# Two transformer blocks on one core: keys transposed once, fewer compressed-score matmuls, a new head, a lag of three

## The chip, the cores and the metric

The kernel runs on one core of a Trainium2 chip. The metric is device time of one execution in microseconds (us); less is better. Below, TensorE is PE in the profile (its weight loads PEld), VectorE is DVE, ScalarE is ACT, GpSimd is POOL and SyncE is SP.

## The reference

256 tokens of 1024 features go through a first block of two layers and a second one of two layers; everything is fp32.

```python
def first_block(x, mem, ...):
    mem_n = rms_norm(mem, mem_norm_g)
    for i in range(2):
        h = rms_norm(x, g_mix_pre[i])
        proj = h @ w_in[i]                       # q 12 heads, k and v 3 heads, 4 memory queries, 64 each
        tok = mixer_a(...) if i == 0 else mixer_b(...)   # banded with sinks | normed, axial rotary, full
        mkv = mem_n @ w_mem_kv[i]
        mo = memory_attention(qm, km, vm)
        x = x + rms_norm(concat(tok, mo) @ w_o[i], g_mix_post[i])
        h = rms_norm(x, g_ffn_pre[i])
        gu = h @ w_gate_up[i]                    # 2 x 2816
        f = (silu(gu[..., :2816]) * gu[..., 2816:]) @ w_down[i]
        x = x + rms_norm(f, g_ffn_post[i])
    return x

def second_block(x, ...):
    for l in range(2):
        x = x + 0.5 * swiglu(rmsnorm(x, ffn1_norm[l]), ...)      # 2816 wide
        h = rmsnorm(x, mix_norm[l]) @ w_in[l]
        h_a, h_b, h_c = split(h)
        o = concat(mla_mixer(h_a), nsa_mixer(h_b), diff_mixer(h_c))   # latent, sparse, differential
        x = x + o @ w_out[l]
        x = x + 0.5 * swiglu(rmsnorm(x, ffn2_norm[l]), ...)
    return rmsnorm(x, final_norm)
```

In `nsa_mixer` each of six query heads scores 15 compressed keys of its group, then all blocks of keys and a window of keys.

## The kernel before

**Numbers.** Every fp32 operand of a product is split into two fp32r tiles, hi and lo, and a product is three matmuls: hi by hi, hi by lo and lo by hi (`mm3`, line 554). A weight unit of 128x1024 numbers comes by DMA from SP into one of three `raw` buffers; ScalarE copies it to `hi`, VectorE subtracts to get `lo` (`load`, line 619), and there are seven pairs of those.

**Two halves.** The tokens are two halves of 128, A and B, each a generator (`script`, line 1485) that asks for weight units in the same order. `drive` (line 1518) gives each unit to A and, `LAG` = 4 units later, to B. Pieces of attention (generators that yield between steps) are advanced once a unit. So while A is at the end of a stage and its norm runs on VectorE and ScalarE, TensorE works on B's last units of the stage before.

**Order of the work.** The program is run once with a `Recorder` (line 98) that notes every engine call with what it reads and writes; `plan` (line 179) lays them out in time with a model of each call's duration (`cost`, line 445) and of the tile slots, and `Replay` (line 399) issues them in that order. So all of the profile's lines of the kernel's body are L417, the helper's. In `plan` each engine takes what is ready in program order (`MODE` = "order"); on VectorE and ScalarE a ready call gives way to one that comes ready soon. `either` lets plan choose between VectorE and ScalarE for a copy. The instructions of `setup` (line 814), among them the identities idf (fp32), idr (fp32r) and idb (bf16), are not in the plan.

**Keys.** `k_split` (line 715) writes hi, lo and hi again side by side, 192 columns a head. `k_stack` (line 725) transposes columns 0 to 127 (hi over lo) and 64 to 191 (lo over hi), two transposes a head, and one copy of 128x256 moves both to SBUF. One matmul of the stacked query (hi over lo) with each stack then gives hi by hi plus lo by lo, and hi by lo plus lo by hi. The second block's sparse keys go the same way in `mix_2`, into `KN`. In `compressed` (line 1280) a head takes two matmuls of 16 columns, one for each stack of `KC`, added up in PSUM on a mask that a matmul of 96 columns has put there.

**The head.** `memory_kv` (line 898) loads 128 rows of `mem` and the gain (512 KB each), multiplies them, transposes the product (`norm_t`, `trsplit`), and projects with `w_mem_kv`. SP issues both loads, and behind them the weight units.

**Ends of a stage.** `add_normed` (line 657) squares the two accumulators on ScalarE, takes the root's reciprocal on GpSimd, and on VectorE scales and adds to x; then `norm_t` multiplies x by the next gain, and PE transposes it. There are four such ends a half in the first block. `add_scaled` (line 665) does the second block's without a norm.

## Time and profile before

| | |
|---|---|
| Runs, us | 1672.1, 1673.17, 1675.07 (median 1673.17) |
| Profiled execution: span from first to last instruction, us | 1670.2 |
| Time of the profiled execution by the clock of the runs | not given beside the span; the median is 3.0 above the span |
| PE busy, us (share of the span) | 1645.6 (99%) |
| DVE, ACT busy | 1031.5 (62%), 895.1 (54%) |
| Mean granted clock of PE | 0.998 |
| Chain of waits that ended last | PE 93%, DVE 3%, DMA 2%, ACT 1%, issue 1% |

A matmul's end in the profile is modelled and reaches into the next one's time, so that what one costs in a row of them is read from start to start. A row with xN is N instructions in succession. The idle time in brackets is that of the engine before the row, with what ended it. The granted clock is 1.00 at 2.4 GHz; 0.50 is 1.2 GHz.

### The profile page before, as it was taken

The numbers are of one execution on the slowest core, as the hardware profiler recorded it, in microseconds if no ns is written. First come the engines' busy times: TensorE is split into PE (matmuls) and PEld (weight loads), VectorE is DVE, ScalarE is ACT, GpSimd is POOL, SyncE is SP. The second block draws the span as 40 slices with busy tenths as digits, with TensorE's granted clock in tenths as the row PEclk, the third lists the DMA queues.
The fourth block names the chain that finished last, engine by engine and source line by source line (L and its number), as shares of the span: only waits on it lengthen the run. The fifth ranks groups of instructions, "written<-read, shape, count | busy, mean of one in ns | idle before, by whom it ended". The sixth has DMA issues, their size and how long they took to land.

```text
span 1670.2 us, 23044 instructions
## 1 busy us (share of the span) xinstructions
PE 1645.6 (99%) x8648; PEld 1381.4 (83%) x8648; DVE 1031.5 (62%) x1731; ACT 895.1 (54%) x1531; POOL 42.1 (3%) x54
## 2 busy tenths in 40 slices
PE   7999999999999999999999999999999999999998
PEld 6888888789788878888899888888888889888886
DVE  6768555586655565554787755546555588765544
ACT  5766444466544354453677644435454477654443
POOL 0000000010000010000000000000000000000000
PEclk9999999999999999999999999999999999999999
DMA  7526665442566556665533366656665543356653
GB/s 256 177 65 178 182 208 187 154 159 77 171 187 204 186 166 190 185 200 180 161 106 115 114 180 185 192 188 178 181 203 183 170 128 119 103 152 181 196 184 106
DMA packets 141970, 277.12 MB, mean 166 GB/s; under 512 B 19681, under 2 KB 49441, under 8 KB 141857
## 3 DMA queue, kind: packets, MB, share of 16 engines
q1 hardware_dynamic: 141856, 275.64, 54.3%
q8 instruction: 68, 1.11, 0.3%
q14 instruction: 46, 0.37, 0.1%
HBM read 274.55 MB, written 1.05 MB: 165 GB/s over the span
## 4 chain that ended last, share of the span: by engine, by line
PE 93%; DVE 3%; DMA 2%; ACT 1%; issue 1%; POOL 0%; SPq 0%; POOLq 0%; ACTq 0%; DVEq 0%
PE acc L417 86%; PE tr L417 7%; DVE lo L417 1%; DVE tmp L417 1%; DMA raw<-in_w_mem_kv 1%; ACT hi L417 1%; DMA qkg<-in_qk_norm_g 0%; DVE tiny L417 0%; POOL tiny L417 0%; DVE x L417 0%; DMA raw<-in_w_in 0%; ACT tmp L417 0%; DMA f<-in_nsa_phi_v 0%; SPq L417 0%; DVE big L417 0%
## 5 line engine op out<-in xcount | busy, mean ns | idle before, releaser
L417 DVE TENSOR_TENSOR lo<-raw,hi 128x1024 fp32r<-128x1024 f32 (+3 forms) x510 | 609.3, 1197 | 499.7 <-ACT hi L417 498.9
L417 PE MATMUL acc<-hi,hT 128*128 128x512 f32 (+4 forms) x2944 | 876.3, 375 | 1.5 <-ACT hi L417 0.5
L417 ACT ACTIVATE hi<-raw 128x1024 fp32r<-128x1024 f32 (+3 forms) x510 | 528.8, 1039 | 602.8 <-PE acc L417 545.7
L417 PEld LDWEIGHTS acc<-hi,hT 128*128 128x128 f32 x2944 | 537.4, 189 | 99.4 <-DVE hT L417 2.6
L417 PE MATMUL acc<-lo,hT 128*128 128x512 f32 (+4 forms) x1472 | 552.2, 376 | 4.2 <-DVE lo L417 3.9
L417 PE MATMUL acc<-hi,big 128*128 128x512 f32 (+1 forms) x1360 | 398.2, 396 | 0.0
L417 PEld LDWEIGHTS acc<-lo,hT 128*128 128x128 f32 x1472 | 277.5, 189 | 52.7 <-DVE lo L417 6.6
L417 PEld LDWEIGHTS acc<-hi,big 128*128 128x128 f32 (+1 forms) x1360 | 251.4, 188 | 51.2 <-ACT big L417 0.3
L417 PE MATMUL acc<-lo,big 128*128 128x512 f32 (+1 forms) x680 | 223.0, 396 | 0.0
L417 ACT ACTIVATE tmp<-acc,tiny 128x256 f32<-128x256 f32 (+4 forms) x272 | 133.9, 502 | 36.7 <-PE acc L417 26.3
L417 PEld LDWEIGHTS acc<-lo,big 128*128 128x128 f32 (+1 forms) x680 | 127.2, 188 | 27.0 <-issue 0.3
L417 PE MATMUL tr<-idf,tmp 128*128 128x128 f32 x796 | 128.0, 275 | 9.6 <-DVE tmp L417 7.5
L417 PEld LDWEIGHTS tr<-idf,tmp 128*128 128x128 f32 x796 | 98.6, 143 | 29.5 <-issue 8.4
L417 ACT ACTIVATE big<-tr 128x512 fp32r<-128x512 f32 (+3 forms) x192 | 88.2, 474 | 49.7 <-PE tr L417 46.1
L417 POOL TENSOR_TENSOR tiny<-tiny,nhalf 128x1 f32<-128x1 f32 (+4 forms) x46 | 39.5, 859 | 1605.4 <-DVE tiny L417 1565.4
L417 DVE TENSOR_TENSOR big<-tr,big 128x512 fp32r<-128x512 f32 (+3 forms) x108 | 61.0, 572 | 16.5 <-ACT big L417 13.1
L417 PE MATMUL acc<-v,tmp 128*128 128x64 f32 x520 | 68.4, 267 | 0.0
L417 PEld LDWEIGHTS acc<-v,tmp 128*128 128x128 f32 x520 | 66.9, 192 | 1.5 <-issue 0.3
L417 DVE SCALAR_TENSOR_TENSOR tmp<-acc,tiny,tmp 128x512 f32<-128x512 f32 x72 | 50.6, 703 | 14.4 <-PE acc L417 13.9
L417 DVE TENSOR_REDUCE tiny<-acc 128x2 f32<-128x512 f32 (+2 forms) x76 | 49.4, 651 | 11.1 <-PE acc L417 9.9
L417 PE MATMUL acc<-big,big 128*128 128x256 f32 (+1 forms) x232 | 45.0, 302 | 0.0
L417 PEld LDWEIGHTS tr<-idr,tmr 128*128 128x128 f32 x340 | 37.0, 142 | 8.1 <-DVE tmr L417 3.5
(134 smaller groups left out, 714.8 us busy)
## 6 DMA issues: line engine op xcount, KB each, us to landing
raw<-in_w_gate_up SPq DMA_DIRECT2D x88, 512.0 KB, 3.7
raw<-in_ffn_wg SPq DMA_DIRECT2D x88, 512.0 KB, 3.7
raw<-in_ffn_wu SPq DMA_DIRECT2D x88, 512.0 KB, 3.7
raw<-in_ffn_wd SPq DMA_DIRECT2D x88, 512.0 KB, 3.3
raw<-in_w_down SPq DMA_DIRECT2D x44, 512.0 KB, 3.4
raw<-in_w_in SPq DMA_DIRECT2D x20, 512.0 KB, 3.7
raw<-in_w_in SPq DMA_DIRECT2D x24, 384.0 KB, 3.3
raw<-in_w_o SPq DMA_DIRECT2D x16, 512.0 KB, 3.3
```

The source lines that it names most:

```text
L417: getattr(getattr(self.nc, eng), name)(*args, **kw)
```

## The change

It has five parts. (1) `k_split` writes hi and lo once; a key head has one transpose, and the new `halves` makes the second stack by copying the upper 64 partitions to the lower ones and the reverse: three copies in place of one. `KN` is filled the same way. (2) `compressed` scores a head with one matmul of 32 columns (both stacks side by side, mask of 192 columns), and VectorE adds the two halves. (3) `memory_kv` loads `mem` and the gain in halves of 256 KB with the first weight unit requested in between, and `script` puts 16 matmuls of idb by idb (256 columns) ahead of everything. (4) `LAG` is 3. (5) `plan` makes four passes. In the first every engine goes by program order; each pass gives every call a latest start, reckoned back from TensorE's sequence without gaps, and in the next VectorE, ScalarE and GpSimd take the ready call with the earliest latest start; the pass with the shortest model time is used. The cost model has new figures for small matmuls and fp32r transposes.

```diff
-LAG = 4
+LAG = 3
-MODE = "order"
+PASSES = 4
+MARGIN = 2000.0
+BY_TIME = ("vector", "scalar", "gpsimd")
...
+    def plan(self, passes=PASSES):
+        best = None
+        latest = None
+        for k in range(passes):
+            order = self.schedule(latest)
+            if best is None or self.makespan < best[0]:
+                best = self.makespan, [(o.i, o.pick) for o in order], dict(self.slot)
+            latest = self.latest_starts(order)
...
+        keys = {e: (lambda i: latest[i]) if latest and e in BY_TIME else (lambda i: i) for e in self.ENGINES}
...
         if name == "transpose":
-            return 56.0 if "float32r" in dt else 109.0
+            return 84.0 if "float32r" in dt else 109.0
         if dt.endswith("float32"):
-            return max(214.5, 4 * n / 2.4 + 2.7)
-        return max(55.0, n / 2.4 + 2.7)
+            return max(111.0, 4 * n / 2.4 + 2.7)
+        if "float32r" in dt:
+            return max(112.0, 6 + 0.4415 * n)
+        return max(50.0, n / 2.4 + 2.7)
...
     def k_split(self, x):
-        kd = self.t("tmp", [nh, 192], F32R)
...
+        kd = self.t("tmp", [nh, 2, 64], F32R)
+        self.split(x, kd[:, :, 0], kd[:, :, 1])
         return kd
+    def halves(self, out, ps):
+        ps = ps.bitcast(F32)
+        self.copy(out[:, 0], ps)
+        self.copy(out[0:64, 1], ps[64:128])
+        self.copy(out[64:128, 1], ps[0:64])
...
         for h in range(nh):
-            for i in range(2):
-                self.nc.tensor.transpose(ps[:, (2 * h + i) * P:(2 * h + i + 1) * P],
-                                         kd[:, h, 64 * i:64 * i + 128], self.idr)
+            self.nc.tensor.transpose(ps[:, h * P:(h + 1) * P], kd[:, h].rearrange("p a b->p (a b)"), self.idr)
         for h in range(nh):
-            self.copy(tiles[h][:, :, j * P:(j + 1) * P],
-                      ps[:, 2 * h * P:(2 * h + 2) * P].bitcast(F32).rearrange("p (a b)->p a b", a=2))
+            self.halves(tiles[h][:, :, j * P:(j + 1) * P], ps[:, h * P:(h + 1) * P])
...
     def memory_kv(self, j):
         m = self.t("gb", [D])
-        self.nc.sync.dma_start(m, self.ins["mem"][0, j * P:(j + 1) * P])
-        hT, r = self.norm_t(m, self.gain("mem", self.ins["mem_norm_g"]))
...
+        for b in range(2):
+            s = slice(b * 512, (b + 1) * 512)
+            self.nc.sync.dma_start(m[:, s], self.ins["mem"][0, j * P:(j + 1) * P, s])
+            if j == 0:
+                self.nc.sync.dma_start(g[:, s], vec[:, s].to_broadcast([P, 512]))
+            if b == 0:
+                first = yield ("w_mem_kv0", 0, 2, 0, 512, P)
+        hT, r = self.norm_t(m, self.gains["mem"])
...
             for h in range(6):
-                for i in range(2):
-                    nc.tensor.matmul(sc[:, h], QB[h // 4][:, h % 4], self.KC[:, h // 3, i],
-                                     start=False, stop=h + i == 6)
+                nc.tensor.matmul(s2[:, h], QB[h // 4][:, h % 4],
+                                 self.KC[:, h // 3].rearrange("p a b->p (a b)"), start=False, stop=h == 5)
+            sc = self.t("sm", [6, 16])
+            nc.vector.tensor_reduce(sc, ps[:, 0:192].rearrange("p (h i c)->p h c i", h=6, i=2), axis=AX.X, op=ALU.add)
...
             self.mem = [self.t("kn", [2, 512]) for _ in range(2)]
+            ps = self.tr()
+            for _ in range(16):
+                self.nc.tensor.matmul(ps[:, 0:256], self.idb, self.idb.unsqueeze(1).to_broadcast([P, 2, P]),
+                                      start=True, stop=True)
         yield from self.memory_kv(j)
```

The order of the instructions shows what this moves, at three places. In it gb0 is the tile of `mem`, gb1 that of the gain, tmp their product or x times the next gain, raw a weight unit, tr a PSUM tile of transposes, hT the split transposed activations, and acc an accumulator.

The first is VectorE at the start of the program. Before:

```order
L823 MEMSET nhalf_73 128x16
L417 TENSOR_SCALAR tiny1_103<-tiny0_101 128x1
L417 TENSOR_TENSOR tmp1_93<-gb0_91,gb1_92 128x512
L417 TENSOR_TENSOR tmp2_97<-gb0_91,gb1_92 128x512
L819 CAST idr_69<-idf_64 128x128
L821 CAST idb_71<-idf_64 128x128
L417 TENSOR_TENSOR lo0_108<-raw0_106,hi0_107 128x1024
```

Now:

```order
L888 MEMSET nhalf_73 128x16
L476 TENSOR_TENSOR tmp0_97<-gb0_92,gb1_93 128x512
L476 TENSOR_TENSOR lo0_96<-raw0_94,hi0_95 128x1024
L884 CAST idr_69<-idf_64 128x128
L886 CAST idb_71<-idf_64 128x128
L476 TENSOR_TENSOR hT1_100<-tr1_98,hT0_99 128x512
L476 TENSOR_TENSOR tmp2_101<-gb0_92,gb1_93 128x512
```

The first lo has moved ahead of the casts that make idr and idb, and one half of the product stands ahead of it.

The second is TensorE at the start. Before:

```order
L417 MATMUL tr0_94<-idf_64,tmp1_93 128x128 x4
L417 MATMUL tr1_98<-idf_64,tmp2_97 128x128 x4
L417 MATMUL acc0_105<-hi0_107,hT0_95 128x512
L417 MATMUL acc0_105<-lo0_108,hT0_95 128x512
L417 MATMUL acc0_105<-hi0_107,hT2_96 128x512
L417 MATMUL acc0_105<-hi0_107,hT0_95 128x512
```

Now the first rows are 16 times a weight load of idb and a matmul, of which the last pair stands here with what follows:

```order
L476 LDWEIGHTS idb_71
L476 MATMUL tr0_91<-idb_71 128x256
L476 MATMUL tr1_98<-idf_64,tmp0_97 128x128 x4
L476 MATMUL acc0_108<-hi0_95,hT0_99 128x512
L476 MATMUL acc0_108<-lo0_96,hT0_99 128x512
L476 MATMUL acc0_108<-hi0_95,hT1_100 128x512
L476 MATMUL acc0_108<-hi0_95,hT0_99 128x512
L476 MATMUL acc0_108<-lo0_96,hT0_99 128x512
```

The transposes of the product, and with them the first projection, have moved behind the matmuls of idb.

The third is VectorE at the end of half B's feed-forward in the first layer, some 330 us into the program, where A has begun the next mixer's projections (lo1 and lo2 before, lo0 now, are of its weights). Before:

```order
L417 SCALAR_TENSOR_TENSOR tmp4_120<-acc5_154,tiny22_179,gb1_92 128x512
L417 SCALAR_TENSOR_TENSOR tmp1_93<-acc4_152,tiny22_179,gb1_92 128x512
L417 TENSOR_SCALAR v10_150<-acc3_151,tiny17_173 128x192
L417 TENSOR_TENSOR x1_79<-x1_79,tmp4_120 128x512
L417 TENSOR_REDUCE tiny3_126<-tmp2_97 128x3
L417 TENSOR_TENSOR x1_79<-x1_79,tmp1_93 128x512
L417 TENSOR_SCALAR tiny1_103<-tiny3_126 128x3
L417 TENSOR_TENSOR tmp6_123<-x1_79,gb0_91 128x512
L417 TENSOR_TENSOR lo1_111<-raw0_106,hi1_110 128x1024
```

Now:

```order
L476 SCALAR_TENSOR_TENSOR tmp2_101<-acc4_152,tiny23_182,gb1_93 128x512
L476 SCALAR_TENSOR_TENSOR tmp4_118<-acc5_160,tiny23_182,gb1_93 128x512
L476 TENSOR_TENSOR x1_79<-x1_79,tmp2_101 128x512
L476 TENSOR_TENSOR x1_79<-x1_79,tmp4_118 128x512
L476 TENSOR_TENSOR tmp0_97<-x1_79,gb0_92 128x512
L476 TENSOR_TENSOR tmp6_121<-x1_79,gb0_92 128x512
L476 CAST big0_145<-tr0_91 64x128
L476 TENSOR_SCALAR tiny1_106<-tiny4_139 128x1
L476 TENSOR_TENSOR lo0_96<-raw2_112,hi0_95 128x1024
```

Both multiplications by the next gain (tmp0, tmp6; before, tmp0 came four rows below the last one shown) have moved ahead of the subtraction that makes the next lo; the scaling into v, a reduction and a small operation have gone from between. On TensorE, B's eight transposes that read them now stand behind A's 24 matmuls of 384 columns; before, 18 matmuls of 512 columns stood in between.

## Rows read from the trace of the kernel before

**Rows 1.** The page: the span, and part 1, busy time of each engine.

```profile
span 1670.2 us, 23044 instructions
...
PE 1645.6 (99%) x8648; PEld 1381.4 (83%) x8648; DVE 1031.5 (62%) x1731; ACT 895.1 (54%) x1531; POOL 42.1 (3%) x54
```

**Rows 2.** The timeline of TensorE: start us, us, engine, line, what, count, of split keys' transposes.

```profile
107.44 0.45 PE L417 MATMUL tr<-idr,tmr 128*128 128x128 f32 x4
107.73 0.69 PE L417 MATMUL acc<-lo,big 128*128 128x512 f32 x2
...
918.64 0.71 PE L417 MATMUL tr<-idr,tmr 128*128 128x128 f32 x6
919.19 0.47 PE L417 MATMUL acc<-hi,big 128*128 128x512 f32 x1
```

**Rows 3.** The same of compressed scores and what follows them.

```profile
898.77 1.49 PE L417 MATMUL tr<-kc,big 128*128 128x16 f32 x12
900.11 0.48 PE L417 MATMUL acc<-kn,big 128*128 128x256 f32 x2
```

**Rows 4.** The timeline of an end of a feed-forward, 604 to 614 us.

```profile
605.77 0.59 ACT L417 ACTIVATE tmp<-acc 128x512 bf16<-128x512 f32 x1
...
607.77 1.09 PE L417 MATMUL acc<-hi,big 128*128 128x512 f32 x4
...
608.70 0.62 PE L417 MATMUL acc<-lo,big 128*128 128x512 f32 x2
...
610.02 1.29 DVE L417 TENSOR_TENSOR tmp<-x,gb 128x512 f32<-128x512 f32 x2
```

**Rows 5.** Groups of ScalarE by form: count | busy us, mean ns | idle before.

```profile
L417 ACT ACTIVATE big<-tr 128x256 fp32r<-128x256 f32 x85 | 30.7, 382 | 14.4 <-PE tr L417 12.3 <-DVE big L417 0.3
...
L417 ACT ACTIVATE big<-tr 128x128 fp32r<-128x128 f32 x12 | 2.9, 274 | 0.8 <-PE tr L417 0.6
```

**Rows 6.** The timeline of the head, 0 to 18 us.

```profile
7.51 1.94 PE L417 MATMUL tr<-idf,tmp 128*128 128x128 f32 x8 [7.51 <-DVE tmp L417]
...
7.96 1.06 ACT L417 ACTIVATE hi<-raw 128x1024 fp32r<-128x1024 f32 x1 [2.73 <-DMA raw<-in_w_mem_kv]
8.02 0.22 DVE L821 CAST idb<-idf 128x128 bf16<-128x128 f32 x1
...
8.93 1.16 ACT L417 ACTIVATE hT<-tr 128x512 fp32r<-128x512 f32 x2
9.05 1.23 DVE L417 TENSOR_TENSOR lo<-raw,hi 128x1024 fp32r<-128x1024 f32 x1 [0.82 <-ACT hi L417]
...
9.56 0.79 PE L417 MATMUL acc<-hi,hT 128*128 128x512 f32 x1
...
12.38 1.05 PE L417 MATMUL acc<-hi,hT 128*128 128x512 f32 x2
...
13.23 0.63 PE L417 MATMUL acc<-lo,hT 128*128 128x512 f32 x1
...
14.81 0.63 PE L417 MATMUL acc<-hi,hT 128*128 128x512 f32 x2
```

**Rows 7.** Windows: stretch, length, busy us by engine, granted clock, DMA share, GB/s.

```profile
0.00:40.00 40.00, 30.38 (x132) 23.81 (x133) 26.40 (x56) 23.95 (x36) 2.90 (x10) 1.00 0.75 255
335.00:340.00 5.00, 4.16 (x16) 2.78 (x14) 3.57 (x14) 1.27 (x4) 0.59 (x1) 0.66 0.64 210
```

**Rows 8.** The timeline of 328 to 342 us; idle before and its releaser in brackets.

```profile
334.27 0.50 PE L417 MATMUL acc<-lo,hT 128*128 128x512 f32 x1 [2.48 <-DVE lo L417]
...
338.44 0.73 PEld L417 LDWEIGHTS tr<-idr,tmr 128*128 128x128 f32 x6 [0.87 <-DVE tmr L417]
...
340.07 1.09 PE L417 MATMUL tr<-idf,tmp 128*128 128x128 f32 x8 [0.76 <-DVE big L417]
```

**Rows 9.** The timeline of the second block's first mixer, 811.5 to 816 us.

```profile
813.13 0.28 PE L417 MATMUL tr<-idr,tmr 128*128 128x128 f32 x1 [0.55 <-DVE tmr L417]
...
813.75 1.09 PE L417 MATMUL tr<-idf,tmp 128*128 128x128 f32 x8 [0.34 <-DVE tiny L417]
```

More of the change, by code (lines that the diff above doesn't have):

```diff
@@ L178, in add, with latest_starts, schedule @@
         return o
-    def plan(self, prio_mode="level"):
+    def plan(self, passes=PASSES):
[6 more added lines that the diff above has]
+            latest = self.latest_starts(order)
+        self.makespan, order, self.slot = best
+        return order
+    def latest_starts(self, order):
+        ops = self.ops
+        after = [list(o.succs) for o in ops]
+        last = {}
+        for o in order:
+            for nm in self.uses[o.i]:
+                t = self.tiles[nm]
+                key = t[0], self.slot[nm]
+                prev = last.get(key)
+                if prev is None or prev[0] != nm:
+                    if prev is not None:
+                        for j in prev[1]:
+                            after[j].append(o.i)
+                    last[key] = nm, [o.i]
+                else:
+                    last[key][1].append(o.i)
+        d = [math.inf] * len(ops)
+        at = 0.0
+        for o in order:
+            if o.eng == "tensor":
+                d[o.i] = at
+                at += o.dur
+        for o in reversed(order):
+            x = d[o.i]
+            for j in after[o.i]:
+                e = ops[j]
+                y = d[j] - LAT(o.eng, e.eng) - o.dur - (DMA_LAT if o.eng == "sync" else 0.0)
+                if y < x:
+                    x = y
+            d[o.i] = x
+        top = at
+        return [min(x, top + o.i) for x, o in zip(d, ops)]
+    def schedule(self, latest):
         ops = self.ops
@@ L197, in plan @@
                     users[a.tensor.name] += 1
[L199 to L207 removed]
+        self.uses = uses
         tags = {}
@@ L267, in plan @@
         future = {e: [] for e in self.ENGINES}
-        key = (lambda i: -lev[i]) if prio_mode == "level" else (lambda i: i) if prio_mode == "order" else prio_mode
+        keys = {e: (lambda i: latest[i]) if latest and e in BY_TIME else (lambda i: i) for e in self.ENGINES}
+        behind, ideal = 0.0, 0.0
         sources = [[] for _ in ops]
@@ L329, in plan @@
                                 break
-                    if ok and e in ("vector", "scalar"):
+                    if ok and latest and e in BY_TIME:
+                        for r, i in heapq.nsmallest(6, future[e]):
+                            if r >= t + o.dur:
+                                break
+                            if ops[i].start is not None or latest[i] >= x[0]:
+                                continue
+                            f_late = t + o.dur - latest[i] - behind + MARGIN
+                            x_late = r + dict(ops[i].alts)[e] - x[0] - behind + MARGIN
+                            if f_late > max(0.0, x_late):
+                                ok = False
+                                wake.append(r)
+                                break
+                    elif ok and e in ("vector", "scalar"):
+                        key = keys[e]
                         for r, i in heapq.nsmallest(4, future[e]):
@@ L632, in load, with proj @@
         return hi, lo
-    def proj(self, hT, key, c0, w, kk, out):
+    def proj(self, hT, key, c0, w, kk, out, first=None):
         for k0 in range(0, 8, kk):
-            hi, lo = yield (key, k0 * P, kk, c0, w, P)
+            if first is None or k0:
+                hi, lo = yield (key, k0 * P, kk, c0, w, P)
+            else:
+                hi, lo = first
             for k in range(kk):
@@ L1578, in plan @@
         n.drive(lag)
-        order = n.rec.plan(MODE)
-        return [(o.i, o.pick) for o in order], [n.rec.slot.get(x, 0) for x in n.rec.names]
+        order = n.rec.plan()
+        return order, [n.rec.slot.get(x, 0) for x in n.rec.names]
 def net(tc, ins, out, lag=LAG):
```

47 lines of the change are left out of this document (21 added, 26 removed).

## The prediction

> **What bounds the kernel now.** I read the head of the profile first. Its span is 1670.2 us and TensorE is busy for 1645.6 of it, while VectorE has 62% and ScalarE 54% [rows 1]. The median of the three runs, 1673.17 us, lies 3.0 us above the span; I sum against the span and add the same 3.0. A kernel with 99% of TensorE busy gains in three ways only: fewer columns on TensorE, less time at the half clock, and less idle time in the few stretches that have any. So I went by windows and timelines to those stretches. There are three that the change touches: the first 40 us, the stretch from 329 to 341 us, and the starts of the second block's mixer, one a layer (the first at 813 us).
>
> **1. TensorE work removed.** Matmul records overlap, so a price is a difference of starts. Six transposes of split keys start at 918.64 and the next matmul at 919.19: 0.55 / 6 = 0.092 us each. Four start at 107.44 and the next group at 107.73: 0.073 us each [rows 2]. The change has 68 of these fewer (272 instead of 340). I take the middle, 0.083: **-5.6 us** (-5.0 to -6.3). Twelve compressed-score matmuls of 16 columns start at 898.77 and what follows starts at 900.11: 0.112 us each, more than a 128-column transpose takes [rows 2, 3]. Half of the 48 go and the others get 32 columns. No row shows 32 columns, but if 128 cost 0.083 to 0.092, 32 should cost no more than 16 did: **-2.7 us** (0, if twice the columns took twice the time, to -2.7). The mask matmul grows by 96 columns four times; 512 columns take (608.70 - 607.77) / 4 = 0.2325 us [rows 4], so 4 x 0.2325 x 96 / 512 = **+0.2 us**.
>
> The Trainium skill (TensorE: Matmul & The Clock Gate, "Wait — 56ns, not 53.3ns?") states a start-to-start of 55.8 ns for 128 columns at the full clock and a floor of about 25 ns for small ones, by which, as an estimate, the removals are worth 68 x 0.056 + 24 x 0.025 = 4.4 us; the trace does not agree, at 0.073 to 0.092 and 0.112 us.
>
> **2. Copies added.** In place of two transposes and one copy of 256 columns (0.382 us on ScalarE), a head has one transpose and three copies; the whole one takes 0.274 us and the half ones at most that [rows 5]. That is at most 0.44 us more for each of 52 heads, 23 us, and some for eight groups of second-block keys. With 38% of VectorE's and 46% of ScalarE's span free [rows 1] I cost it at nothing: TensorE has the other half's weights to work on in between. If that cover went, 23 us would stand on the path. The compressed scores' extra reduction, four times, is in the same position.
>
> **3. The head, 0 to 40 us.** The new idle matmuls are first in TensorE's queue, but the order of the changed kernel shows that they are not early. They need idb. Its cast now stands on VectorE behind the subtraction that makes the first lo, which needs the first weights and ScalarE's hi; before, both casts stood ahead of it. The real transposes stand behind all 16 idle matmuls, and ScalarE's third instruction, hT, waits for those, with the later hi behind it, so the raw buffers are held and SP's queue stops too. Before, hi began at 7.96 when the weights had landed, lo at 9.05, and the first projection matmul at 9.56 [rows 6]. Now the first weights follow two half loads on SP, not two whole ones; I take them at 6.7 (6.0 to 7.96). Then hi 1.06, lo 1.23 and two casts of 0.22 give 9.4. Early matmuls run at half pace, which is 1.2 GHz of 2.4: 12.38 to 13.23 for two of 512 columns, 0.425 each [rows 6]; so 256 columns take 0.21 and 16 of them 3.4: 12.8. Four transposes at half pace (half of 1.94) and a hT (half of the 1.16 that the two took) follow, so the first projection comes at 14.4 instead of 9.56.
>
> It is not all lost. Before, TensorE was busy 30.38 us of the first 40 [rows 7], but from 7.51 on its matmuls stepped at 0.425, until about 14.6: the four from 13.23 to 14.81 make three such steps and a shorter one [rows 6]. The windows give a mean clock of 1.00 for these 40 us [rows 7]; I go by the steps, and count these 7 us as half. Full-pace work done: 30.4 - 3.5 = 26.9. Now it starts at 14.4 with the clock already full and more weights landed: 40 - 14.4 - 0.7 of small waits = 24.9. So **+2.0 us**. Bounds: weights at 6.0 and no wait at all, -0.1 or so; weights at 7.96 and some 2.1 us of waits, +4.7. A gain needs the idle matmuls to start early, which is a rival below.
>
> **4. 329 to 341 us.** Here half B ends a feed-forward while TensorE works on half A's next projection. On VectorE the subtraction for A's weights stands behind B's additions and a multiplication; TensorE waits 2.48 us for it, until 334.27. Then the granted clock falls: mean 0.66 between 335 and 340, one part at full and 3.4 us at half, which loses 1.7 us. Two more waits, 0.87 (weight load at 338.44) and 0.76 (340.07), end it [rows 7, 8]. Together 5.8 us. In the new order VectorE has both multiplications ahead of that subtraction, and TensorE has B's eight transposes right behind A's 24 matmuls of 384 columns, so nothing of 512 columns waits there for lo. What remains is B's own chain: on the pattern of 605.77 (second square) to 610.02 plus 1.29 (last multiplication), 5.5 us after its last matmul [rows 4], against 24 x 0.174 = 4.2 us of cover (0.174 is 384 / 512 of 0.2325). 5.5 - 4.2 = 1.3, of which some 1.1 shows, since four of the transposes need only the first multiplication. So 5.8 - 1.1: **-4.7 us** (-5.8, or nothing if the stall moves).
>
> **5. Starts of the second block's mixer.** TensorE waits 0.55 for VectorE's tmr at 813.13 and 0.34 at 813.75 [rows 9]: that subtraction stands behind the two long multiplications. The new order has it ahead of them and B's transposes earlier. Twice 0.9: **-1.8 us** (0 to -2.6, if the smaller waits after it go too).
>
> **6. Lag three instead of four.** At an end of a feed-forward, A's chain (squares, scale, additions, multiplications) runs while TensorE works on B's last units. The orders count 26 matmuls of B between A's last one and A's first transposes before, and 23 after: 23 x 0.2325 = 5.35 us, against a chain of 5.5 to the second multiplication [rows 4]. At the four ends with a normed addition I cost 0.25 us each: **+1.0 us** (0 to +1.4). What is late next there is only the second half of hT.
>
> Sum: -5.6 - 2.7 + 0.2 + 2.0 - 4.7 - 1.8 + 1.0 = **-11.6**. Span 1658.6; time 1673.2 - 11.6 = **1661.6 us**.
>
> **Rivals.** (a) *The idle matmuls work as meant*: TensorE starts before the weights land, the half-pace spell is spent on them, and the first real matmul, no later than 9.56, runs at the full clock. The 3.5 us of part 3 come back: -3.5 in place of +2.0, 1656.1. For it: the cast of idb took 0.22 and needs only idf, which the transposes at 7.51 already read [rows 6]. Against it: the order on VectorE. The Trainium skill ("TensorE: Matmul & The Clock Gate", "Why this matters for your kernels") advises matmuls as a warm-up ahead of those that count; by that rule this rival is the outcome, and the trace agrees that early matmuls run at half pace, but no run here shows idle matmuls.
>
> (b) *The reordering does nothing on the chip*: the planner's times are a model's, and the stall of part 4 may only move to another piece of VectorE's queue. Then parts 4 and 5 give nothing: 1661.6 + 6.5 = 1668.1. For it: a queue that is busy 71% of the time there (3.57 of 5 us, [rows 7]) has little room for what is put off.
>
> (c) *Slower: lag three leaves the four normed ends without cover.* If A's chain, stretched by B's subtractions on VectorE, comes 2.5 us late, TensorE waits as it did at 334.27 and the clock falls as it did there: 2.5 + 1.7 = 4.2 us an end [rows 7, 8]. Less than 2.8 such ends leave a gain; three bring the kernel level (1661.6 + 12.6 = 1674.2) and four make it 1678.4. For it: the sums in part 6 are within 0.2 us of each other. Against it: on VectorE the order stt, stt, add, add, mult, mult has nothing between, so the chain should not stretch by more than one subtraction, 1.23.
>
> (d) *The copies of part 2 are late*: if each of some 12 bunches of heads made TensorE wait 0.4 us, 1661.6 + 4.8 = 1666.4.
>
> (e) *Small matmuls cost only their columns.* Then what the rows show between their starts is largely the neighbours', and stays when they go: 512 columns in 0.2325 make 128 cost 0.058 and 16 cost 0.007, and the removals bring 68 x 0.058 + 24 x 0.007 = 4.1 in place of 8.3: 1665.8. Against it: six and twelve in a row, at 0.092 and 0.112 [rows 2, 3]. The page named in part 1 is nearest to this rival.
>
> **How the numbers follow.** Chances: the forecast 0.58, (a) 0.10, (b) 0.14, (c) 0.07, (d) 0.08, (e) 0.03. The range is **1654 to 1669**: its low end is (a) with the upper bounds of parts 4 and 5, its high end (b) with 1 us on top; it leaves out (c) and some of (b) with a bad head. A measurement of this kernel tells about 0.2%, 3.3 us, from no change. Everything except (c) and the worst mixture of (b) with the head's +4.7 is below 1669.8: faster 0.90; level with three bad ends, or that mixture, 0.05; slower 0.05.
>
> **What would show it.** Right: first instruction of TensorE near 9.4 us, first projection near 14.4, right after a cast of idb; no wait of over 1.5 us and no half clock between 320 and 345; no wait for tmr at the second block's mixer; compressed matmuls still near 0.11 us apart. Wrong: idle matmuls that begin before 7 us (a); a wait for lo of over 2 us anywhere behind a feed-forward (b); waits for tmp with a granted clock of half at the ends of feed-forwards (c); many waits for big (d).

## The result, and the profile after

The changed kernel takes 1689.53 us (median of four runs, 1685.93 to 1693.87), the kernel before in the same comparison 1672.63 (1670.45 to 1675.07). The ratio is 1.0105, with a 95% interval of 1.0092 to 1.0118: one per cent slower, above the range of the prediction, which had it faster.

The head of the page of the changed kernel, to be set beside [rows 1]:

```profile
span 1690.5 us, 23001 instructions
...
PE 1651.1 (98%) x8572; PEld 1381.4 (82%) x8572; DVE 1036.5 (61%) x1758; ACT 911.1 (54%) x1628; POOL 41.9 (2%) x54
```

TensorE has 5.5 us more busy time, although 92 small matmuls went and 16 idle ones came (68 + 24 - 16 = 76 fewer in all), and 39.4 us without a matmul where before had 24.6. Some of the busy time is slow time: the mean granted clock of the span fell from 0.998 to 0.994, so (0.998 - 0.994) x 2 x 1690.5 = 13.5 us more stood at the half clock, and half of that, 6.8 us, was lost. Two of the four runs (1685.93 and 1686.78) had mean clocks of 0.999 and 0.998 and are still 13 and 14 us above the kernel before, so that this half clock makes the difference to the other two runs (1692.27, the profiled one, and 1693.87) and not the bulk of the loss.

What TensorE waited for, largest first (view of waits, changed kernel; columns: who for whom, us in total, times, longest):

```profile
PE tr L476 <- DVE idb L886: 10.3, 1, 10.3
PE tr L476 <- DVE tmr L476: 6.3, 8, 2.0
PE acc L476 <- ACT hT L476: 4.3, 7, 1.4
PE tr L476 <- DVE tmp L476: 2.6, 4, 1.4
PE tr L476 <- ACT big L476: 1.7, 4, 0.5
...
PE tr L476 <- DVE big L476: 1.0, 2, 0.5
```

The first row is the head. Below it there is no large wait but a crowd of small ones, behind tmr, hT, tmp and big; all those that the view lists come to 30.0 us, against 16.5 before. To see where they stand I compared the starts of the same weight units on TensorE in both traces. The changed kernel is 5.4 us behind at the tenth unit (the head), 10.9 behind at the end of the first mixer, 14.8 after the second, still 14.9 when the second block begins, 19.6 after that block's first mixer and 20.3 at the end. The loss beyond the head is in three of the four mixers; feed-forwards lose nothing. Windows over the head and two mixers, first of the changed kernel, then of the kernel before (columns as in [rows 7]):

```profile
0.00:40.00 40.00, 26.34 (x120) 19.49 (x120) 22.05 (x46) 19.79 (x29) 2.36 (x9) 1.00 0.73 244
325.00:400.00 75.00, 68.60 (x394) 58.47 (x393) 60.05 (x141) 54.81 (x141) 11.04 (x10) 0.95 0.40 125
860.00:935.00 75.00, 72.77 (x484) 65.78 (x483) 60.61 (x192) 55.97 (x184) 3.12 (x3) 0.95 0.32 95
```

```profile
325.00:400.00 75.00, 70.91 (x463) 62.84 (x464) 63.23 (x148) 53.52 (x134) 9.79 (x9) 0.98 0.42 133
860.00:935.00 75.00, 74.42 (x533) 67.06 (x532) 59.55 (x166) 50.89 (x149) 2.05 (x2) 1.00 0.38 117
```

In both mixers TensorE does less in the same 75 us, at a lower clock, while ScalarE is busier by 1.3 and 5.1 us. (The changed kernel is 11 to 15 us behind there, so its windows hold partly other work; the loss itself is read from the starts above.) In the first 40 us 26.34 takes the place of 30.38, and 3.59 of it are idle matmuls.

The head of the changed kernel (timeline; what answers to [rows 6]):

```profile
7.70 1.06 ACT L476 ACTIVATE hi<-raw 128x1024 fp32r<-128x1024 f32 x1 [5.68 <-DMA raw<-in_w_mem_kv]
8.78 1.23 DVE L476 TENSOR_TENSOR lo<-raw,hi 128x1024 fp32r<-128x1024 f32 x1 [1.70 <-ACT hi L476]
...
10.06 0.22 DVE L886 CAST idb<-idf 128x128 bf16<-128x128 f32 x1
...
10.34 3.59 PE L476 MATMUL tr<-idb 128*128 128x256 bf16 x16 [10.34 <-DVE idb L886]
...
13.72 0.68 PE L476 MATMUL tr<-idf,tmp 128*128 128x128 f32 x4
...
15.09 0.50 PE L476 MATMUL acc<-hi,hT 128*128 128x512 f32 x1 [0.69 <-ACT hT L476]
...
18.34 0.50 PE L476 MATMUL acc<-lo,hT 128*128 128x512 f32 x1 [0.65 <-DVE lo L476]
```

The cast of idb ends at 10.3 and TensorE begins there. The idle matmuls run at the half pace ((13.72 - 10.34) / 16 = 0.21 from start to start), the transposes stand behind them, and the first projection matmul comes at 15.09 instead of 9.56.

The copies of part 2, in the first mixer (timeline, ScalarE and VectorE rows of 40.8 to 44.2 us):

```profile
40.87 1.99 ACT L476 ACTIVATE big<-tr 128x128 fp32r<-128x128 f32 x7
...
42.89 0.28 DVE L476 CAST big<-tr 64x128 fp32r<-64x128 f32 x1 [1.25 <-ACT big L476]
...
43.21 0.28 ACT L476 ACTIVATE big<-tr 128x128 fp32r<-128x128 f32 x1 [0.35 <-DVE big L476]
...
43.52 0.29 DVE L476 CAST big<-tr 64x128 fp32r<-64x128 f32 x1 [0.34 <-ACT big L476]
...
43.85 0.27 ACT L476 ACTIVATE big<-tr 64x128 fp32r<-64x128 f32 x1 [0.36 <-DVE big L476]
```

The copies of one head alternate between partitions 0 to 127, the lower 64 and the upper 64, and they do not overlap. Seven in a row take 1.99 us (a row names the form of its first one), so they start (1.99 - 0.28) / 6 = 0.285 us apart, which is the whole duration of one (0.274, [rows 5]). Where the halves of a head go to different engines it is worse: from 42.89 to 43.85 four copies alternate between VectorE and ScalarE, the last three each waiting 0.34 to 0.36 for the other engine. Before, a head was one copy, and two in a row (timeline of the kernel before)

```profile
331.33 0.65 ACT L417 ACTIVATE big<-tr 128x256 fp32r<-128x256 f32 x2
```

stand 0.65 - 0.382 = 0.27 us apart, less than the 0.382 that one takes ([rows 5]): those overlap. So a head costs 3 x 0.285 = 0.86 us of one engine's time instead of 0.27. The planner's `cost` had such a copy at 0.158 us on ScalarE, 0.47 for a head.

How that reaches TensorE is seen best in the second mixer (timeline of the changed kernel, rows of the chain only):

```profile
357.37 1.72 ACT L476 ACTIVATE big<-tr 128x128 fp32r<-128x128 f32 x6
...
358.82 0.61 DVE L476 CAST big<-tr 64x128 fp32r<-64x128 f32 x2 [0.84 <-ACT big L476]
...
359.46 0.27 ACT L476 ACTIVATE big<-tr 64x128 fp32r<-64x128 f32 x1 [0.37 <-DVE big L476]
...
359.75 0.84 ACT L476 ACTIVATE tmp<-acc,tiny 128x256 f32<-128x256 f32 x2
...
360.48 0.41 ACT L476 ACTIVATE tmr<-tmp 128x256 fp32r<-128x256 f32 x1
...
360.96 0.42 DVE L476 TENSOR_TENSOR tmr<-tmp,tmr 128x256 fp32r<-128x256 f32 x1
...
361.43 0.53 PE L476 MATMUL tr<-idr,tmr 128*128 128x128 f32 x4 [2.03 <-DVE tmr L476]
```

Six copies hold ScalarE for 1.72 us; two more on VectorE and a last one on ScalarE follow; only then come the two scalings of accumulators into tmp, then tmr on ScalarE and on VectorE, and the four transposes that read tmr start 2.03 us late. Nothing in these rows waits for the copied keys. What is late is the work that was queued behind the copies on ScalarE and VectorE.

### The profile page after: what moved, and what is told of

It reads as the page before. It is cut to its first block, busy times and chain, and to the rows that moved or that the text cites. A ratio compares the mean times of both kernels' runs of the same rounds, so it can differ in the third digit from the quotient of the medians.

```text
span 1690.5 us, 23001 instructions
## 1 busy us (share of the span) xinstructions
PE 1651.1 (98%) x8572; PEld 1381.4 (82%) x8572; DVE 1036.5 (61%) x1758; ACT 911.1 (54%) x1628; POOL 41.9 (2%) x54
## 4 chain that ended last, share of the span: by engine, by line
PE 88%; DVE 5%; ACT 3%; DMA 1%; issue 1%; POOL 0%; POOLq 0%; SPq 0%; ACTq 0%; DVEq 0%
PE acc L476 81%; PE tr L476 7%; DVE lo L476 1%; DVE tmp L476 1%; ACT big L476 1%; ACT hi L476 1%; DMA raw<-in_w_in 1%; ACT tmp L476 1%; DVE big L476 1%; DVE x L476 1%; DVE tiny L476 0%; POOL tiny L476 0%; DMA raw<-in_w_mem_kv 0%; DMA raw<-in_ffn_wu 0%; DVE hT L476 0%
## 5 line engine op out<-in xcount | busy, mean ns | idle before, releaser
L476 ACT ACTIVATE big<-tr 64x128 fp32r<-64x128 f32 (+4 forms) x269 | 107.1, 406 | 62.1 <-PE tr L476 45.9
L476 DVE SCALAR_TENSOR_TENSOR tmp<-acc,tiny,tmp 128x512 f32<-128x512 f32 (+1 forms) x72 | 50.7, 704 | 18.7 <-PE acc L476 18.7
L476 PEld LDWEIGHTS tr<-idr,tmr 128*128 128x128 f32 x272 | 30.7, 141 | 15.1 <-DVE tmr L476 10.5
```

Source lines behind the costliest of these rows:

```text
L476: getattr(getattr(self.nc, eng), name)(*args, **kw)
```

## The experiments

Fifteen kernels, all against the kernel before. Its median was 1671.3 or 1671.4 us in each of these comparisons. The letters in the expectations stand for the theories as they are put there. The order below is by question, not by time. Every edit makes the planner order the whole program anew, so a difference between two kernels is that of the edit and of the two orders together; how much the order alone can do is measured under the lag.

**Is it the planner's passes?** The changed kernel with one pass, so that every engine goes by program order again.

```diff
-PASSES = 4
+PASSES = 1
```

> The changed kernel with one pass of the planner, so that every queue goes by program order as before; the new costs, keys, head and lag stay. Theory P: the 14 us of the mixers come back, and the head may too, 1670 to 1676. Theories K and L: within 3 us of the changed kernel, 1687 to 1693.

1690.06 us, ratio 1.0114 (1.0098 to 1.0129): the same as the changed kernel. At this lag the passes neither lose nor bring anything that can be measured.

**Is it the keys?** The changed kernel with the keys of before: two transposes and one copy a head. Lag, passes, head and compressed scores stay as changed.

```diff
-    def halves(self, out, ps):
...
+            for i in range(2):
+                self.nc.tensor.transpose(ps[:, (2 * h + i) * P:(2 * h + i + 1) * P], kd[:, h, 64 * i:64 * i + 128], self.idr)
...
-            self.halves(tiles[h][:, :, j * P:(j + 1) * P], ps[:, h * P:(h + 1) * P])
+            self.copy(tiles[h][:, :, j * P:(j + 1) * P],
+                      ps[:, 2 * h * P:(2 * h + 2) * P].bitcast(F32).rearrange("p (a b)->p a b", a=2))
```

> The changed kernel with the keys made as before: two transposes a head and one copy. TensorE has its 68 transposes back, 5.6 us. Theory K: the waits of the mixers go, 14 us, so 1690 + 5.6 - 14 = 1681. Theories L and P: the waits stay, 1690 + 5.6 = 1695.

1673.63 us, 1.0019 (1.0008 to 1.0029). So the new keys cost 16.9 - 2.3 = 14.6 us, each against the kernel before it was compared with, although they take 68 transposes, 5.6 us by the prediction's price, off TensorE. By this pair the copies therefore cost about 20 us. TensorE's waits come to 20.5 us in all, of 30.0 in the changed kernel; those for tmr go from 6.3 to 1.7, those for hT only from 4.3 to 3.5. Of the wait of 2.03 at 361.43 about half stays (1.04, at 353.15 in this kernel), so only the other half is the copies'. The windows of the two mixers in this kernel:

```profile
325.00:400.00 75.00, 72.15 (x463) 62.62 (x462) 63.81 (x150) 55.00 (x129) 11.10 (x10) 1.00 0.41 130
860.00:935.00 75.00, 74.76 (x540) 67.16 (x540) 61.67 (x182) 53.36 (x163) 2.63 (x2) 1.00 0.37 118
```

The clock is full again and TensorE's busy time is above that of before in both.

**The keys alone.** The kernel before with nothing but the new keys.

```diff
-            self.copy(tiles[h][:, :, j * P:(j + 1) * P], ...
+            self.halves(tiles[h][:, :, j * P:(j + 1) * P], ps[:, h * P:(h + 1) * P])
```

> The kernel before with the new keys alone: one transpose and three copies a head. Theory K: -5.6 us of transposes and about +14 us of waits, 1672.6 + 8 = 1681. Theories L and P: the copies are covered, 1672.6 - 5.6 = 1667.

1706.41 us, 1.0204 (1.0187 to 1.0221): 35 us slower. The mean clock of the span is 0.988, that is (0.998 - 0.988) x 2 x 1705 = 34 us more at the half clock, 17 lost by it; the rest is waiting. The same windows:

```profile
325.00:400.00 75.00, 66.01 (x360) 56.01 (x358) 61.12 (x146) 46.01 (x111) 10.42 (x9) 0.91 0.42 134
860.00:935.00 75.00, 68.37 (x397) 60.26 (x396) 50.63 (x159) 47.66 (x145) 3.08 (x3) 0.84 0.28 91
```

**Is it the hops from engine to engine?** The same kernel, but the three copies of a head go to one engine, ScalarE and VectorE by turns.

```diff
+        self.side = 1 - getattr(self, "side", 1)
+        for o, i in ((out[:, 0], ps), (out[0:64, 1], ps[64:128]), (out[64:128, 1], ps[0:64])):
+            if self.side:
+                self.nc.vector.tensor_copy(o, i)
+            else:
+                self.nc.scalar.activation(o, i, AF.Copy)
```

> The kernel before with the new keys alone, as e4, but the three copies of a head all go to one engine, VectorE and ScalarE by turns, where e4 left each copy to the planner. In the order of e4, 158 copies from tr wait for the other one of the two engines, against 62 before; here it is 98. Theory H (the copies are cheap, but copies of one head on two engines wait for one another, 0.3 us a hop, and TensorE then waits for the bank): 36 of 96 added waits stay, so 1671.3 + 35 x 36 / 96 = 1684. Theory W (three short copies of 0.27 to 0.29 us where one of 0.38 was, whatever the engine): as e4, 1703 to 1709.

1687.64 us, 1.0096 (1.0081 to 1.0111): 19 us less. The expectation puts that down to the hops, but this kernel has an order of its own too, and with a mean clock of 0.992 instead of 0.988 some 7 of the 19 are clock; the time alone doesn't show what a hop costs. The same edit in the changed kernel:

> The changed kernel with the three copies of a head on one engine, VectorE and ScalarE by turns. Against e3 the new keys cost 16 us net, so 21.6 us of waits beside the 5.6 us that they save. Theory H: two thirds of the waits go, as from e4 to e5, 1690 - 12 = 1678. Theory W: 1687 to 1693.

1686.0 us, 1.0092 (1.0076 to 1.0107), only some 3 us less than the changed kernel, between the two expectations and nearer to the one by which the copies' own time is what costs. In the changed order, then, the hops are the smaller part.

**Is it that the planner did not know?** The planner is given the durations of the trace, 0.305 us on VectorE and 0.285 on ScalarE, and the three copies as a chain.

```diff
+                op.alts = [("vector", 190.0 + w), ("scalar", 170.0 + w)]
+                if last is not None:
+                    op.preds[last] = True
```

> The changed kernel, where the planner reckons each copy of a key half at what the traces show (0.285 us on ScalarE, 0.305 on VectorE for 128 columns) and takes the three copies of a head to follow one another. Same instructions. Theory B (the loss is the planner's: it puts copies ahead of work that TensorE waits for since it thinks them cheap): 1675 to 1681. Theory C (the copies' time itself is what lacks, whatever the order): 1686 to 1692.

1689.3 us, 1.011 (1.0093 to 1.0128): nothing. The planner's ignorance is not the cause; it finds no better place for them.

**Is it the change of partitions?** One engine for a group of heads, and the copies grouped: first the whole copies, then all that write the lower half, then all that write the upper one. The copies are the same ones as in the one-engine kernel before it; partitions change less often, and the engines now take turns by group and not by head.

```diff
+        for k in range(3):
+            for h in range(nh):
+                self.part(tiles[h][:, :, j * P:(j + 1) * P], ps[:, h * P:(h + 1) * P], k)
```

> As e12 (the copies of a head on one engine, by turns), and where two heads are copied together, both whole copies first, then both lower halves, then both upper ones: three changes of partition for two heads, not six. By the traces two heads then take about 3 x 0.157 + 3 x 0.29 = 1.3 us in place of 1.73. Theory: 1686 - 4 to 6 = 1681. If changes of partition don't matter: 1686.

1679.82 us, 1.0047 (1.0033 to 1.0061): 6 us less than with one engine, 10 less than the changed kernel. In the first mixer (timeline of this kernel):

```profile
40.93 1.34 ACT L476 ACTIVATE big<-tr 128x128 fp32r<-128x128 f32 x6
...
41.42 1.49 DVE L476 CAST big<-tr 128x128 fp32r<-128x128 f32 x6
```

ScalarE's six copies of two heads start (1.34 - 0.28) / 5 = 0.21 us apart instead of 0.285. By single records the three steps that stay on their partitions take 0.156, 0.177 and 0.174 us and the two that change them 0.301 and 0.273. VectorE's, in its own row, take 0.201, 0.215 and 0.208 against 0.295 and 0.300. So the same copies overlap where they stay on their partitions. It isn't the tile that keeps them apart: at both changes the next copy goes to the tile of another head. The kernel is faster as expected; how much of the 6 us comes from the turns by group was not tested.

**Is it the lag?** The kernel before with a lag of three; the kernel before with the new keys and a lag of three; the changed kernel with a lag of four; and that with the keys of before.

```diff
-LAG = 4
+LAG = 3
```

> The kernel before with a lag of three alone. If the lag of three is a gain by itself, as it was at the changed planner (e8 to e3: 27 us): below 1668. If it only undoes what the new figures or the new keys did: 1670 to 1676; part 6 of the prediction, 0 to 1.4 us for the ends of feed-forwards, lies there too. Theory Q: 1680 or more, since any other order fits worse.

1679.47 us, 1.0055 (1.0039 to 1.0072), 8 us slower, between the expectations. At three ends of a stage TensorE waits 0.97, 1.15 and 1.17 us for hT (133.19, 419.25 and 611.68).

> The kernel before with the new keys and a lag of three, no more. With the rest of the change, going from four to three took 22 us off (e1). Theory G (a shorter lag holds one pair of hi and lo fewer, so that more weights are ready when VectorE and ScalarE are late with copies; the planner has no part in it): 1706 - 20 = 1686. If the planner's passes are what makes use of the lag: 1700 or more.

1690.08 us, 1.0111 (1.0096 to 1.0126): with the new keys, a lag of three gains 16 us.

> The changed kernel with a lag of four units again, all else kept. Against the kernel before, the changed one is 19.9 us late at the end of TensorE's work, and progress through the weight units puts that loss at 10.9 us up to the end of the first mixer (5.4 of it in the head), 3.9 in the second mixer, 4.7 in the second block's first mixer. Theory L (the lag: one unit less of the other half's work lies under each piece's chain, so transposes wait for tmr): the 14 us of the mixers come back, 1676. Theory K (the copies that make the second key stack are on the path): no more than 3 us come back, 1687 to 1690. Theory P (the queues ordered by latest start put off what TensorE waits for): as K, 1687 to 1690.

1711.49 us, 1.0242 (1.0227 to 1.0257). All theories had 1676 to 1690, and all missed.

> The changed kernel with the old keys and a lag of four. Theory G (a short lag only makes up for late copies): without the new keys the lag is worth little, 1671 to 1677. If the lag of three is a gain by itself, as it was with the new keys: 1690 or more.

1700.85 us, 1.0173 (1.0157 to 1.0189). So in the changed program a lag of four loses 27 us against a lag of three without the new keys too: it isn't the new keys that make it bad there. What is left that differs from the kernel before, which does well at four, is the cost figures, the passes, the compressed scores and the head. The cost figures alone, then: the kernel before, the same instructions, with the changed figures for TensorE in the planner.

```diff
-            return 56.0 if "float32r" in dt else 109.0
+            return 84.0 if "float32r" in dt else 109.0
...
+        if "float32r" in dt:
+            return max(112.0, 6 + 0.4415 * n)
```

> The kernel before with the new cost figures of TensorE alone (fp32r transposes at 84 ns, small matmuls at about 111): the same instructions, another order. Theory Q (with a lag of four the order of before is one that happens to fit, and a plan from other figures puts VectorE and ScalarE late by some us in the mixers, where TensorE's clock then falls): 1685 to 1700, with 10 us or more at half clock. Theory R (the figures are nearer to the chip, so the order is no worse): 1668 to 1674.

1696.76 us, 1.0153 (1.0138 to 1.0168): 25 us slower from the order alone. Windows:

```profile
325.00:400.00 75.00, 69.53 (x419) 59.88 (x418) 59.95 (x137) 50.20 (x116) 8.59 (x9) 0.98 0.40 134
860.00:935.00 75.00, 69.92 (x458) 62.52 (x456) 53.23 (x161) 46.63 (x141) 3.00 (x3) 0.91 0.29 95
```

The figures that are nearer to the chip (0.084 for a transpose, by [rows 2]) give a worse order. So the order of the kernel before fits the chip better than its planner can know, and any edit that makes it plan again can lose that. What in that order is so good was not found. Where it is good shows in the starts of TensorE's matmuls of lo, counted through: the kernel with the cost figures alone is 6.9 us behind at 780 us and 22.6 at 1000, and the one with the lag alone goes from 1.8 ahead to 9.0 behind. Both lose most in the second block's first mixer.

With that, the price of the keys can be read from four pairs of kernels that differ in the keys alone. The changed kernel and the one with the old keys give 14.6; at a lag of three with the old figures it is 1690.08 - 1679.47 = 10.6; at a lag of four with the new ones 1711.49 - 1700.85 = 10.6. The pair with the kernel before gives 35, but there the good order is lost as well, and that alone was 25. So the keys cost 10.6 to 14.6 us, and the copies, with the 5.6 for the transposes, 16 to 20.

**What does the head cost?** The changed kernel with the keys of before and the head of before (whole loads, no idle matmuls).

```diff
-            for _ in range(16):
-                self.nc.tensor.matmul(ps[:, 0:256], self.idb, ...
...
-        for b in range(2):
-            s = slice(b * 512, (b + 1) * 512)
-            self.nc.sync.dma_start(m[:, s], self.ins["mem"][0, j * P:(j + 1) * P, s])
+        self.nc.sync.dma_start(m, self.ins["mem"][0, j * P:(j + 1) * P])
```

> The changed kernel with the keys and the head of before; it keeps the compressed scores, the lag of three and the planner. Theory: the new head costs what progress through the first weight units showed, 5.4 us, and nothing of it is made good later: 1673.6 - 5.4 = 1668. Rival: the head is made good by 40 us, as the prediction had it but for 2 us: 1671.6.

1668.59 us, 0.9979 (0.9969 to 0.9989): faster than the kernel before, and 5.0 us less than with the new head. TensorE's largest waits in this kernel:

```profile
PE tr L476 <- DVE tmp L476: 8.0, 3, 7.5
PE acc L476 <- ACT hT L476: 3.6, 5, 1.9
PE tr L476 <- DVE tmr L476: 2.1, 5, 1.2
```

7.5 of the first row is the start, as before. All that the view lists comes to 16.0 us, against 16.5 before: the wait of 2.48 for lo [rows 8] is gone, and the 3.6 for hT stand in its place, 1.85 of them in one wait at 34.63. Behind that wait the clock falls, as it did behind the other (windows of 35 to 40 and of 325 to 345 us):

```profile
35.00:40.00 5.00, 4.71 (x21) 3.99 (x21) 4.39 (x12) 4.03 (x10) 0.55 (x1) 0.68 0.63 199
325.00:345.00 20.00, 19.57 (x110) 17.02 (x109) 18.55 (x40) 12.68 (x24) 4.26 (x4) 1.00 0.39 118
```

So a stall with its spell at the half clock moved from 334 us to 34 us.

**Can the idle matmuls be early?** The kernel with the keys of before, and idb made by GpSimd in the way idf is, instead of by VectorE's cast.

```diff
-        nc.vector.tensor_copy(self.idb, self.idf)
+        make_identity(nc, self.idb)
```

> e3 (old keys, new head) with idb made by GpSimd like idf, in place of VectorE's cast of idf: the 16 idle matmuls can start at about 2 us and end at 5.5, before the first product at 6.4. Rival (a) of the prediction: the head's 5.0 us come back and the half-pace spell of 3.5 us goes: 1673.6 - 8.5 = 1665. Alternative: the clock has fallen again by the time that the first weights are there, or weights set the pace: 1668 to 1670.

1670.04 us, 0.9993 (0.9983 to 1.0002): 3.6 less than with the late ones. TensorE at the start (timeline):

```profile
1.71 3.23 PE L476 MATMUL tr<-idb 128*128 128x256 bf16 x16 [1.71 <-POOL idb masks.py:199]
6.22 0.66 PE L476 MATMUL tr<-idf,tmp 128*128 128x128 f32 x4 [1.28 <-DVE tmp L476]
8.97 0.79 PE L476 MATMUL acc<-hi,hT 128*128 128x512 f32 x1 [2.10 <-ACT hT L476]
9.75 0.79 PE L476 MATMUL acc<-lo,hT 128*128 128x512 f32 x1
```

And the window of 8 to 16 us:

```profile
8.00:16.00 8.00, 7.03 (x20) 5.03 (x21) 6.28 (x11) 6.77 (x10) 1.11 (x2) 0.58 1.01 375
```

The idle matmuls run from 1.71 to 4.9 and bring the clock to full at 4.4 us. But then TensorE has only the four transposes until 8.97, and at 7.8 the clock falls back for 6.8 us (0.58 in the window; the mean clock of the ten runs of this kernel lies between 0.994, the profiled one, and 0.999, so not every run has this fall): the first two real matmuls start 0.78 apart, slower even than the 0.425 of the half pace [rows 6]. So the spell was bought and not used. The last kernel fills the hole as well: 29 idle matmuls instead of 16, and eight fp32 ones of the first product behind the first transposes, into the same unused tile.

```diff
-            for _ in range(16):
+            for _ in range(29):
...
+                for _ in range(8):
+                    self.nc.tensor.matmul(self.warm[:, 0:128], self.idf, xn[:, 0:128], start=True, stop=True)
```

> e11 (old keys, idb by GpSimd, new head) with 29 idle matmuls in place of 16, and 8 fp32 ones of the first product behind the first transposes, so that TensorE has no longer gap from 1.7 us until the first projection at 9. Theory: the clock, which in e11 was full from 4.4 us and half again from 7.8 for 6.8 us, stays full, and 3 us come back: 1670.0 - 3 = 1667, which would be faster than both kernels. Alternative: the weights set the pace there and it is made up of waits: 1669 to 1671.

1667.37 us, 0.9977 (0.9968 to 0.9986), as expected: faster than the kernel before and than the changed one, and level with the one with the old head, 1.2 us away. Its start:

```profile
1.71 5.51 PE L476 MATMUL tr<-idb 128*128 128x256 bf16 x29 [1.71 <-POOL idb masks.py:199]
7.06 0.60 PE L476 MATMUL tr<-idf,tmp 128*128 128x128 f32 x4
7.49 1.95 PE L476 MATMUL tr<-tmp,idf 128*128 128x128 f32 x16
9.20 0.48 PE L476 MATMUL acc<-hi,hT 128*128 128x512 f32 x1
9.52 0.45 PE L476 MATMUL acc<-lo,hT 128*128 128x512 f32 x1
```

The first two real matmuls are 0.32 apart, and from 10.54 on they step by 0.23: the full clock is there before the weights' work. It stays until about 37 us and falls then for 3.4 us, behind a wait of 1.73 for hT at 34.90 (0.66 in a window of 36 to 41 us).

## Why the prediction was wrong

**Part 2 failed, and it was nearly all of it.** It costed the copies "at nothing: TensorE has the other half's weights to work on in between", from the busy shares of VectorE and ScalarE over the span. The runs show 16 to 20 us (10.6 to 14.6 for the keys as a whole, and the 5.6 that was costed for the transposes), not far from the 23 that the same paragraph gave if that cover went. Two things were wrong in the step. The price set durations against a duration, 3 x 0.274 - 0.382 = 0.44 a head "at most"; but the copies of before overlap, 0.27 from start to start, and I did not ask whether the new ones would. They don't, so a head takes 0.86 - 0.27 = 0.59 us more of an engine, and 0.44 was no bound. And the question was put to the wrong reader: TensorE does have other work while the keys are copied, and waits for big only 1.7 + 1.0 us. What loses its cover is what stands behind the copies on ScalarE and VectorE, tmr, tmp and hT, which TensorE does wait for. Free time of 46% over the span says nothing of a mixer, where copies come in bunches and ScalarE was busy for 53.52 of 75 us already.

Rival (d), late copies, came nearest and was sized at 12 bunches x 0.4 = 4.8 us, a quarter to a third of what they cost. Its sign, many waits for big, did not come (six, 2.7 us in all): it saw neither the queue behind a bunch nor the clock, which falls at such waits and took 6.8 us of the profiled run.

On the behaviour itself the Trainium skill (VectorE: DVE Perf Modes, "Two Vector instructions with no wait between them") has a rule that I didn't weigh: an instruction whose operands start in another quadrant of partitions than those of the last one is held until the earlier Vector instructions have finished. The trace agrees for VectorE: in the grouped kernel its copies start 0.295 and 0.300 us after the one ahead, which lasts 0.28 to 0.29, where the partitions change, and 0.201 to 0.215 after it where they don't. ScalarE, of which that section does not speak, does the same at 0.285.

**Part 1 held.** In the changed kernel six compressed-score matmuls of 32 columns take 0.82 us by the record at 920.21, and start 0.112 us apart by single records: what 16 columns took [rows 3]. Rival (e) is not needed; but I can't separate the 5.6 us of the transposes from the copies by a run, since they go together.

**Part 3 was right in its reading and short in its size.** The order of VectorE's queue gave 9.4 for the first idle matmul and 14.4 for the first projection; they came at 10.34 and 15.09, since the first weights landed at 7.70, not at 6.7. It costed 2.0 us, and the bound was 4.7; the runs give 5.0 (1673.63 - 1668.59). What was sized too small is the waits behind it: 2.6 us from 15.09 to 40 (24.9 us, of which TensorE is busy for 22.3), 0.65 for lo at 18.34 and 1.39 for hT at 39.31 among them, where the sum had 0.7. Rival (a) is what the idle matmuls could do and did not in this order. Made early they bring 3.6, made early and kept going 6.3 us (1673.63 - 1667.37), against the late ones; against the head of before the first is 1.4 us slower and the second 1.2 faster, where the rival had 3.5. The Trainium skill (TensorE: Matmul & The Clock Gate, "Why this matters for your kernels") advises both halves of this, a warm-up and no idle gap after it; the two runs agree, and here the second half is the one that was easy to miss.

**Parts 4 and 5 came true where they were looked for, and were given back elsewhere.** In the kernel with the old keys and the old head the clock is full from 325 to 345 us, TensorE is busy for 19.57 of these 20, and nothing waits for tmr where the second block's mixers begin. But that kernel should then have gained 2.5 + 4.7 + 1.8 - 1.0 = 8.0 us, and it gains 2.8: the sum of its waits is that of before, with hT at 34.63 in the place of lo at 334.27, and the half clock behind it. That is rival (b), for this much of the change. In the changed kernel itself the stall stands at 342.46 as 1.38 us for tmp, with the half clock behind it.

**Part 6** was small, but twice what was costed: at the four ends in the changed kernel TensorE waits for hT for 0.99 (143.71), 0.30 (335.86), 0.37 (436.92) and 0.31 us (628.57), 2.0 in all against 1.0. In the kernel with the lag alone three of these waits come to 3.3, and most of its 8 us lies elsewhere. Rival (c), four ends at 4.2 us, did not come.

By the runs, then, the loss of 16.9 us is 14.6 for the keys (20 less the 5.6 of the transposes), 5.0 for the head, and -2.8 for all the rest, taken away in this order; by the other pairs the keys are 10.6.

**What stays open:** why the order of before does well at a lag of four, where the orders that came of the new cost figures lose 25 and 27 us. For the run with the cost figures alone some 8 of the 25 us are the half clock; the rest is waits in the mixers, the second block's first one above all, and no single wait stands out there.

## What to carry to other kernels

Before an instruction of a saturated engine is traded for several on engines that look half free, read the start-to-start time of the new instructions in a row and on the partitions that they will have, and ask who stands behind them in the queue; busy shares over the span answer neither. Idle matmuls for the clock need an operand that is ready early, and enough behind them to last until the real work. And where a planner orders the program, replan the old instructions once before judging an edit: here a change of the cost figures alone moved the time by 1.5%.

## What the runs showed of the hardware

Copies on ScalarE that start on other partitions than the one before them do not overlap with it: 0.285 us apart at a duration of 0.274, against 0.16 to 0.18 apart for the same copies where the partitions stay (single records of the grouped kernel), and 0.27 at a duration of 0.382 for those of 256 columns. VectorE's are 0.295 to 0.300 apart where the partitions change, 0.20 to 0.215 where they stay. A copy of 64 partitions is no cheaper than one of 128. The rows by form of the changed kernel (columns as in [rows 5]):

```profile
L476 ACT ACTIVATE big<-tr 64x128 fp32r<-64x128 f32 x70 | 19.0, 271 | 11.8 <-DVE big L476 11.1
...
L476 ACT ACTIVATE big<-tr 128x128 fp32r<-128x128 f32 x53 | 14.2, 278 | 8.1 <-PE tr L476 6.6 <-DVE big L476 1.1
...
L476 DVE CAST big<-tr 64x128 fp32r<-64x128 f32 x34 | 9.7, 288 | 13.9 <-ACT big L476 13.2 <-PE tr L476 0.3
```

Copies of one head that alternate between the engines start 0.31 to 0.33 us apart (42.89 to 43.85), so each pays the whole duration of the one ahead and a hop. And small waits cost more than themselves: in the kernel with the keys alone the half clock made some 17 of the 35 us lost.
